# Two modulation dots per swiglu tile behind the tile's low part, one per output tile, their loads on GpSimd's queue

## The chip, the cores and the metric

The program runs on one core of one Trainium2 chip. The metric is the device time of one execution in microseconds; the profile's span is the time from the first to the last instruction of one execution. TensorE does the matmuls, VectorE, ScalarE and GpSimd the elementwise work, and DMA queues move the data: SP's queue (SyncE) here carries nearly all loads, GpSimd's queue the indirect ones.

## What is computed

Two model blocks on 512 tokens of width 1024. The first has two layers (a gated linear attention, then a latent attention), each followed by a swiglu; the second has a pooling branch beside a convolution branch, and then a layer that picks experts. Each layer is modulated by a vector `mod` that comes from the condition `c` alone, not from the tokens. Cut to what matters here:

```python
D_FF = 2816
for i in range(2):
    mod = c_act @ ada_w[i] + ada_b[i]                 # c_act = silu(c), 1024 -> 6144
    sh1, sc1, g1, sh2, sc2, g2 = jnp.split(mod, 6, axis=-1)
    x = x + g1[:, None, :] * mixer_i(modulate(x, norm_mix[i], sh1, sc1))
    h = modulate(x, norm_ffn[i], sh2, sc2)
    gate, up = jnp.split(h @ ffn_w_in[i], 2, axis=-1)
    x = x + g2[:, None, :] * ((silu(gate) * up) @ ffn_w_out[i])
# the second block begins with mod = silu(c_2) @ ada_w_2 + ada_b_2
```

## The kernel before

The tokens lie along the free dimension: an activation is eight tiles of 128 x 512. A matmul with full precision is made of three in float32r (`mm3`, L274 to L276): activations and weights are each split into a high and a low part, the high part by a ScalarE cast, the low part by a VectorE subtraction (`split`, L240). Weights come in units of 128 x 2048 (`raw<-wst`, 1 MB, from SP's queue, two buffers); each unit is cut into two halves, `whi` and `wlo`, with four buffers each. One unit holds 16 blocks of 128 x 128.

A swiglu (`ffn`, twice in the program) runs in two halves of eleven hidden tiles. For each tile TensorE makes the gate and the up product (8 blocks each, so one unit of weights and 48 matmuls), ScalarE takes the silu of the gate (L739), VectorE multiplies it with the up product (`s`, L741), ScalarE makes the high part `fh` and VectorE the low part `fl` (both L240). Then follow the output tiles of that half: each sums eleven k (33 matmuls), in the order of the hidden tiles, and VectorE adds the result to x (`residual`, L448). The first half has eight output tiles. The second half has six, then `tail` makes the last two with the norm of the next layer, in two halves of the tokens, and `ahead` begins the next layer's matmuls, with the weight low parts on GpSimd.

The modulation vectors are no matmuls: each column of 128 values is one VectorE instruction over 128 x 1024 with an accumulated sum (L312, a dot; `dot`), on a tile `araw` of 0.5 MB that has two buffers. `ada` (L314 to L324) is a generator that does one load and one dot at each `step()`. It is side work: layer 0's last piece (8 dots) and all of layer 1 (48 dots) run beside the first swiglu, those of the second block (48) beside the second swiglu; `silu_c(1)` loads c_2 into the buffer `sc` of the dots and takes its silu on ScalarE (L306, L307) once layer 1's dots have read it. The steps of one kind run in order, each dot in VectorE's program order.

The order of the instructions on each engine is fixed when the program is built, by a scheduler that goes by program order and by a simulated readiness; `tc.issue_after(ins)` forces what a block issues on the engine of `ins` to stand behind it. Before, each tile calls three steps, whose dots have to stand only behind the norm's last instruction, so the scheduler places them by itself.

Of the kernel before, what the change touches and what calls it, by code (L numbers as in the profile page):

```python
# [17 lines left out]
ALU = mybir.AluOpType  # L18
# [3 lines left out]
P = 128  # L22
# [38 lines left out]
ST = (3, 2, 2)  # L61
ARAW = 2
APART = 4
FST = 3
SPILL = [NA // 2 + (2 * i + 1) * (P // 2 - NA // 2) // (2 * NSP) for i in range(NSP)]
LAST = 2
GSC = 2.0 ** 14
# [126 lines left out]
def block_kernel(ctx, tc, x_in, cs_in, wst, vec, cst, gmask, smask, pos, ada1, ada2, wgate, keys, ust, uex, vex, out):  # L194
    nc = tc.nc
    V, A_, T_, G_, SP = nc.vector, nc.scalar, nc.tensor, nc.gpsimd, nc.sync
# [10 lines left out]
    def bank(tag="mm"):  # L207
        return ps.tile([P, S], F32, tag=tag, bufs=4, name=tag)
# [17 lines left out]
    x = [keep.tile([P, S], F32, name=f"x{k}") for k in range(KD)]  # L226
# [10 lines left out]
    state = {"i": 0, "pre": [], "ahead": 0}  # L237

    def split(hi, lo, src, eng=None):
        state["split"] = (A_.copy(hi, src), (eng or V).tensor_sub(lo, src, hi.bitcast(F32)))  # L240
# [16 lines left out]
    def blk(name, n=1, eng=None):  # L257
        while SEQ[state["i"]][0] == "pad":
            state["i"] += 1
        i = state["i"]  # L260
        assert SEQ[i][0] == name, (SEQ[i], name)
        u, o = divmod(i, UB)
        assert o + n <= UB
        if state.get("u") != u:
            with tc.high_priority(state["ahead"]):
                raw = wp.tile([P, UB * P], F32, tag="raw", bufs=RAW, name="raw")
                SP.dma_start(raw, wst[u])
                state["w"] = parts(raw, G_ if name in POOL_LO else eng)
            state["u"] = u
        state["i"] = i + n  # L270
        return part(state["w"], o * P, n * P)

    def mm3(out_, wh, wl, ah, al, first, last):
        T_.matmul(out_, wh, ah, start=first, stop=False)  # L274
        T_.matmul(out_, wh, al, start=False, stop=False)  # L275
        state["mm"] = T_.matmul(out_, wl, ah, start=False, stop=last)  # L276
# [4 lines left out]
    def ahead(name, ah, al):  # L281

        ws = [[blk(name, eng=G_) for _ in ah] for _ in range(4)]
        pre = [bank("mm" if i < 3 else "acc") for i in range(4)]
        for half in range(2):
            cs = halves(half)
            for p, w in zip(pre, ws):
                for k, (wh, wl) in enumerate(w):
                    mm3(p[:, cs], wh, wl, ah[k][:, cs], al[k][:, cs], k == 0, k == len(ah) - 1)
        state["pre"] = pre  # L290

    def proj(name, ah, al, tag="mm"):
        if state["pre"]:
            return state["pre"].pop(0)
        p = bank(tag)
        n = len(ah)
        for k in range(n):
            wh, wl = blk(name)
            mm3(p, wh, wl, ah[k], al[k], k == 0, k == n - 1)
        return p  # L300
# [9 lines left out]
    def dot(out_, w, sc, op=V.scalar_tensor_tensor):  # L310

        op(out=w, in0=w, scalar=1.0, in1=sc, op0=ALU.mult, op1=ALU.mult, accum_out=out_)  # L312

    def ada(l, w, sc, bias, pieces=range(6)):  # L314

        for p in pieces:
            for n in range(p * KD, (p + 1) * KD):
                raw = mn.tile([P, D], F32, tag="araw", bufs=ARAW, name="araw")
                SP.dma_start(raw, w[n * P:(n + 1) * P, :])
                dot(mods[l][:, n:n + 1], raw, sc)  # L320
                if n % KD == KD - 1:
                    m = mods[l][:, p * KD:(p + 1) * KD]
                    V.tensor_add(m, m, bias[:, p * KD:(p + 1) * KD])
                yield  # L324
# [3 lines left out]
    def step(n=1):  # L328
        for _ in range(n):
            next(side["g"], None)  # L330

    def rest():
        for _ in side["g"]:
            pass
# [97 lines left out]
    def tail(name, ah, al, gate, sqs, norm):  # L432

        ws = [[blk(name) for _ in ah] for _ in range(2)]
        for half in range(2):
            cs = halves(half)
            for i, w in enumerate(ws):
                n = KD - 2 + i
                p = bank()
                for k, (wh, wl) in enumerate(w):  # L440
                    mm3(p[:, cs], wh, wl, ah[k][:, cs], al[k][:, cs], k == 0, k == len(ah) - 1)
                residual(n, p, gate, cs)
                for sq, scale in sqs:
                    sq.add(x[n], scale=scale and scale(n), half=half)
            norm(half)

    def residual(n, p, gate, cs=slice(0, S)):
        V.scalar_tensor_tensor(x[n][:, cs], p[:, cs], gate[:, n:n + 1], x[n][:, cs], op0=ALU.mult, op1=ALU.add)  # L448

    def output_norm(name, ah, al, gate, gain, shift, first):  # L450

# [12 lines left out]
    with tc.tile_pool(name="st", bufs=1, reuse_waits="tile") as st, tc.high_priority(2 * AHEAD):  # L464
# [42 lines left out]
        def weights():  # L507
            with ExitStack() as s:
                for eng in (A_, G_):
                    if eng in last:  # L510
                        s.enter_context(tc.issue_after(last[eng].ins))
                state["split"] = None
                w = [blk("gla_w_in", eng=G_) for _ in pre]
                if state["split"]:
                    last[A_], last[G_] = state["split"]
            return w
# [10 lines left out]
        w = weights()  # L527
# [9 lines left out]
        for k in range(KD):  # L537
# [11 lines left out]
            w = w_  # L549
# [4 lines left out]
    with tc.tile_pool(name="gla", bufs=1, reuse_waits="tile") as gp:  # L554
# [19 lines left out]
        p = proj("gla_w_in", hh, hl)  # L574
# [4 lines left out]
        def gates():  # L579

            az, mz = [], []
            for h in range(GLA_H):
                z = bank("acc")
                T_.matmul(z, wg[:, h * P:(h + 1) * P], glr, start=True, stop=True)
                bg = vc("gla_b_gate", h)
                a = gp.tile([P, S], F32, tag="b", bufs=4, name="az")
                m = gp.tile([P, S], F32, tag="vn", bufs=8, name="mz")
                A_.activation(a, z, AF.Abs, bias=bg)
                V.tensor_scalar(m, z, bg, 0.0, op0=ALU.add, op1=ALU.min)
                az.append(a)  # L590
                mz.append(m)
            for a in az:
                e = A_.activation(a, a, AF.Exp, scale=-1.0)
            with tc.issue_after(e.ins):
                for h in range(GLA_H):
                    n = A_.activation(az[h], az[h], AF.Ln, bias=1.0)
                    V.tensor_sub(mz[h], mz[h], az[h])
                    V.tensor_tensor_scan(az[h], smk, mz[h], 0.0, op0=ALU.mult, op1=ALU.add)
            return az, n
# [102 lines left out]
        bs, n = gates()  # L702
        for what in GLA_ORDER.split():
# [8 lines left out]
            elif kind == "r":  # L712
                p = proj("gla_w_in", hh, hl)
# [15 lines left out]

    def ffn(l, sqs, norm, first):  # L730
        gate = mods[l][:, 40:48]
        norm_ = state["norm"]
        with tc.tile_pool(name=f"ffn{l}", bufs=1, reuse_waits="tile") as fp:
            for half in range(2):
                fh, fl = [], []
                for i in range(11):
                    p = proj("ffn_w_in", hh, hl)
                    s = fp.tile([P, S], F32, tag="s", bufs=2, name="s")
                    A_.activation(s, p, AF.Silu)  # L739
                    p = proj("ffn_w_in", hh, hl)  # L740
                    V.tensor_mul(s, s, p)  # L741
                    a = fp.tile([P, S], F32R, name=f"fh{i}")
                    c = fp.tile([P, S], F32R, name=f"fl{i}")
                    split(a, c, s)
                    fh.append(a)
                    fl.append(c)
                    with tc.issue_after(norm_.ins):
                        step(FST)
                for n in range(KD - 2 * half):
                    residual(n, proj("ffn_w_out", fh, fl), gate)  # L750
                    if half:
                        for sq, scale in sqs:
                            sq.pool = sq.pool or fp
                            sq.add(x[n], scale=scale and scale(n))
            rest()
            tail("ffn_w_out", fh, fl, gate, sqs, norm)
            ahead(first, hh, hl)
# [207 lines left out]
    for half in range(2):  # L965
        cs = halves(half)
# [5 lines left out]
    with tc.tile_pool(name="b2", bufs=1, reuse_waits="tile") as bp:  # L972
# [4 lines left out]
        for n in range(4):  # L977
            p = proj("w_in_2", hh, hl)
# [5 lines left out]
        for n in range(4):  # L984
            p = proj("w_in_2", hh, hl)
# [34 lines left out]
        for g in range(4):  # L1020
            p = proj("w_in_2", hh, hl)
            step(4)
            w = WINDOWS[g]
# [20 lines left out]
        for n in range(16):  # L1044
            p = proj("w_in_2", hh, hl)
# [10 lines left out]
        for g in range(4):  # L1056
            p = bank("mm")
# [26 lines left out]
        for n in range(8):  # L1084
            p = proj("pool_up_2", ph_, pl_)
            V.tensor_mul(sg[n], sg[n], p)
        for n in range(8):
            p = proj("conv_out_2", ch_, cl_)
# [9 lines left out]
    with tc.tile_pool(name="peer", bufs=1, reuse_waits="tile") as pp:  # L1098
# [38 lines left out]
        with tc.tile_pool(name="sel", bufs=1, reuse_waits="tile") as sp:  # L1137
# [179 lines left out]
            for h in range(PH):  # L1317
                qq, ql = [], []
                for half in range(2):
                    p = proj("w_query_2", hh, hl)  # L1320
                    t = sp.tile([P, 3 * P], F32, tag="q", bufs=4, name="q")
                    A_.copy(t, p[:, :S - P])
                    l = sp.tile([P, P], F32, name=f"ql{h}_{half}")
# [3 lines left out]
                for c in range(NT - 1):  # L1327
                    cs = slice(c * P, (c + 1) * P)
# [21 lines left out]
        with tc.tile_pool(name="exp", bufs=1, reuse_waits="tile") as ep:  # L1350
# [81 lines left out]
            for g in range(P // GJ):  # L1432
# [13 lines left out]
                for half in range(2):  # L1446
# [12 lines left out]
                    for dd in range(4):  # L1459
                        n = half * 4 + dd  # L1460
# [95 lines left out]
```

## Time and profile before

| | |
|---|---|
| median of three runs | 2837.29 us (2834.54 to 2839.94) |
| the profiled execution | 2844.19 us, span 2842.3 us |
| TensorE busy | 2716.3 us (96%) |
| VectorE busy | 2109.8 us (74%) |
| ScalarE busy | 1070.5 us (38%) |
| GpSimd busy | 704.0 us (25%) |
| DMA moved | 560.62 MB, 197 GB/s in the mean |
| first swiglu, from the first product to its norm | about 338 to 685 us |
| second swiglu | about 944 to 1290 us |

Times are those of one profiled execution unless a run is named. Busy time of TensorE is modelled: the durations of its matmuls overlap, so the rate is read from the distance between the starts of neighbouring rows. In a timeline's row, the square bracket gives the idle time of the engine just before the instruction and what ended it. In a list of waits, the columns are the waiting instruction, what it waited for, the total in us, how often, and the longest.

### The profile page before, as it was taken

The page shows a single profiled execution, that of the slowest core. Times are in us where ns is not written, and L with a number is a line of the kernel's source. Part 1 is how long each engine was busy: PE and PEld are TensorE (multiplying, and loading weights), DVE is VectorE, ACT ScalarE, POOL GpSimd, SP SyncE. Part 2 cuts the span into 40 slices and gives each one's busy share as a digit, 9 for nine tenths or more (in the row PEclk, how much of TensorE's full clock was granted, in tenths as well). Part 3 has the DMA queues.
Part 4 walks back from the last instruction along what each step waited for, and adds up shares of the span by engine and source line. Part 5 has one row for each costly group of instructions (what it writes and reads, how often), then busy time and mean ns, then how long its engine had stood idle before and what let it go on. Part 6 is the DMA issues. An engine that isn't in the chain of part 4 may idle for free. (4 is left out here: it accounts for less than half of the span.)

```text
span 2842.3 us, 38989 instructions
## 1 busy us (share of the span) xinstructions
PE 2716.3 (96%) x14889; PEld 2441.4 (86%) x14889; DVE 2109.8 (74%) x4011; ACT 1070.5 (38%) x1530; POOL 704.0 (25%) x556
## 2 busy tenths in 40 slices
PE   6789998999999999999999999998899999999998
PEld 4677887888778878888888889998899999999998
DVE  8874766435776774337966798888989898988986
ACT  4443322222433322233453336653333333333332
POOL 4541100001011000001521420003545455444550
PEclk9899999999999999999999999999999999999999
DMA  6441477422211674232223236656999998998993
GB/s 267 139 137 62 148 259 256 142 95 88 75 45 60 210 264 148 89 104 76 89 89 104 77 120 214 210 196 241 337 340 359 355 340 328 341 344 320 350 344 131
DMA packets 184363, 560.62 MB, mean 197 GB/s; under 512 B 13248, under 2 KB 66912, under 8 KB 157680
## 3 DMA queue, kind: packets, MB, share of 16 engines
q1 hardware_dynamic: 142352, 407.08, 40.9%
q0 software_dynamic: 41472, 151.01, 14.3%
q8 instruction: 117, 1.92, 0.3%
q14 instruction: 70, 0.57, 0.1%
q10 hardware_dynamic: 352, 0.03, 0.0%
HBM read 527.32 MB, written 30.75 MB: 196 GB/s over the span
## 5 line engine op out<-in xcount | busy, mean ns | idle before, releaser
L240 ACT CAST whi<-raw 128x1024 fp32r<-128x1024 f32 x510 | 535.6, 1051 | 1171.4 <-PE mm L275 689.7
L275 PE MATMUL mm<-hl,whi 128*128 128x512 f32 (+2 forms) x2544 | 899.8, 355 | 8.9 <-DVE hl L426 8.1
L274 PE MATMUL mm<-hh,whi 128*128 128x512 f32 (+2 forms) x2544 | 899.7, 355 | 2.7 <-ACT hh L425 2.0
L276 PE MATMUL mm<-hh,wlo 128*128 128x512 f32 (+2 forms) x2544 | 898.8, 354 | 0.1
L240 DVE TENSOR_TENSOR wlo<-raw,whi 128x1024 fp32r<-128x1024 f32 x472 | 580.2, 1230 | 296.8 <-ACT whi L240 288.0
L275 PEld LDWEIGHTS mm<-hl,whi 128*128 128x128 f32 x2544 | 482.4, 190 | 57.4 <-DVE hl L426 9.8
L274 PEld LDWEIGHTS mm<-hh,whi 128*128 128x128 f32 x2544 | 482.5, 190 | 49.5 <-ACT hh L425 2.6
L276 PEld LDWEIGHTS mm<-hh,wlo 128*128 128x128 f32 x2544 | 482.8, 190 | 48.2 <-issue 1.5
L240 POOL TENSOR_TENSOR wlo<-raw,whi 128x1024 fp32r<-128x1024 f32 x38 | 90.7, 2391 | 908.7 <-ACT whi L240 864.0
L1377 POOL DMA_INDIRECT rows<-vex,eidx x144 | 215.2, 1494 | 214.4 <-DVE y L1391 198.1
L1377 POOL DMA_INDIRECT rows<-uex,eidx x144 | 210.1, 1459 | 214.2 <-DVE rows L1381 164.9
L312 DVE SCALAR_TENSOR_TENSOR araw<-araw,sc 128x1024 f32<-128x1024 f32 x128 | 160.6, 1258 | 98.0 <-DMA araw<-ada 97.4
L1391 DVE SCALAR_TENSOR_TENSOR y<-rows,act,y 128x1024 f32<-128x1024 f32 x142 | 181.7, 1280 | 7.3 <-DMA rows<-vex,eidx 6.7
L1381 DVE SCALAR_TENSOR_TENSOR rows<-rows,hn 128x1024 f32<-128x1024 f32 x144 | 170.1, 1220 | 14.8 <-DMA rows<-uex,eidx 14.8
L274 PE MATMUL mm<-fh,whi 128*128 128x512 f32 (+1 forms) x396 | 147.5, 372 | 11.3 <-ACT fh L240 11.3
L275 PE MATMUL mm<-fl,whi 128*128 128x512 f32 (+1 forms) x396 | 147.7, 373 | 1.7 <-DVE fl L240 1.7
L276 PE MATMUL mm<-fh,wlo 128*128 128x512 f32 (+1 forms) x396 | 146.9, 371 | 0.0
L1310 ACT ACTIVATE stage<-acc 128x512 f32<-128x512 f32 x92 | 91.6, 1105 | 37.0 <-PE acc L1307 26.6
L1307 PE MATMUL acc<-oa,ob 128*128 128x128 f16 x736 | 101.5, 296 | 0.3 <-DVE oa L1298 0.2
L274 PEld LDWEIGHTS mm<-fh,whi 128*128 128x128 f32 x396 | 76.2, 192 | 24.6 <-ACT fh L240 12.1
L448 DVE SCALAR_TENSOR_TENSOR x<-mm,mod,x 128x512 f32<-128x512 f32 (+1 forms) x66 | 43.9, 666 | 62.8 <-PE mm L276 62.7
L275 PEld LDWEIGHTS mm<-fl,whi 128*128 128x128 f32 x396 | 76.1, 192 | 15.3 <-DVE fl L240 2.7
(1381 smaller groups left out, 4593.9 us busy)
## 6 DMA issues: line engine op xcount, KB each, us to landing
raw<-wst SPq DMA_DIRECT2D x127, 1024.0 KB, 4.9
araw<-ada SPq DMA_DIRECT2D x128, 512.0 KB, 4.6
raw<-ust SPq DMA_DIRECT2D x64, 1024.0 KB, 6.4
raw<-vex SPq DMA_DIRECT2D x64, 1024.0 KB, 7.6
gd<-stage SPq DMA_DIRECT2D x23, 1024.0 KB, 4.5
gt<-gd SPq DMA_DIRECT2D x16, 1472.0 KB, 9.4
aw<-ada SPq DMA_DIRECT2D x16, 512.0 KB, 8.9
spilled<-a SPq DMA_DIRECT2D x24, 184.0 KB, 3.1
```

Source lines behind the costliest of these rows:

```text
L240: state["split"] = (A_.copy(hi, src), (eng or V).tensor_sub(lo, src, hi.bitcast(F32)))
L274: T_.matmul(out_, wh, ah, start=first, stop=False)
L275: T_.matmul(out_, wh, al, start=False, stop=False)
L276: state["mm"] = T_.matmul(out_, wl, ah, start=False, stop=last)
L312: op(out=w, in0=w, scalar=1.0, in1=sc, op0=ALU.mult, op1=ALU.mult, accum_out=out_)
L448: V.scalar_tensor_tensor(x[n][:, cs], p[:, cs], gate[:, n:n + 1], x[n][:, cs], op0=ALU.mult, op1=ALU.add)
L1307: T_.matmul(p[:, t * P:(t + 1) * P], ob[:, q, :, t], oa[i][:, q, :, t], start=i == 0, stop=i == 1)
L1310: A_.mul(st[:, :, t1:t1 + 4].rearrange("p j t -> p t j"), p.rearrange("p (t j) -> p t j", t=4), 1.0 / GSC)
L1377: G_.indirect_dma_start(out=r, out_offset=None, in_=uex if up_ else vex, in_offset=bass.IndirectOffsetOnAxis(ap=eidx[:, n:n + 1] if n < P ...
L1381: V.scalar_tensor_tensor(r, r, 1.0, hn if n < P else hx, op0=ALU.mult, op1=ALU.mult, accum_out=act[:, n:n + 1])
L1391: V.scalar_tensor_tensor(z, r, act[:, n:n + 1], z, op0=ALU.mult, op1=ALU.add)
```

## The change

Three edits. In a swiglu tile, two steps instead of three (`FST`), and their dots now stand behind the tile's own low part `fl` (the VectorE half of `split`) instead of the norm. Each output tile, except the last two, which `tail` makes, gets one step behind its residual. The loads of `ada` for layer 1 and for the second block go to GpSimd's queue; those of layer 0 stay on SP's.

```diff
-FST = 3
+FST = 2
@@ ada
-                SP.dma_start(raw, w[n * P:(n + 1) * P, :])
+                (G_ if l else SP).dma_start(raw, w[n * P:(n + 1) * P, :])
@@ residual
-        V.scalar_tensor_tensor(x[n][:, cs], p[:, cs], gate[:, n:n + 1], x[n][:, cs], op0=ALU.mult, op1=ALU.add)
+        return V.scalar_tensor_tensor(x[n][:, cs], p[:, cs], gate[:, n:n + 1], x[n][:, cs], op0=ALU.mult, op1=ALU.add)
@@ ffn
-        norm_ = state["norm"]
...
-                    with tc.issue_after(norm_.ins):
+                    with tc.issue_after(state["split"][1].ins):
                         step(FST)
                 for n in range(KD - 2 * half):
-                    residual(n, proj("ffn_w_out", fh, fl), gate)
+                    r = residual(n, proj("ffn_w_out", fh, fl), gate)
+                    with tc.issue_after(r.ins):
+                        step()
```

The lines after it move up by one in `ffn` (L741 becomes L740) and down by one behind it.

VectorE at the end of the first half of the first swiglu, before. `fl_3222` is tile 9's low part, `L741` the product of tile 10, `fl_3298` tile 10's low part; `L312` is a dot:

```order
L240 TENSOR_TENSOR fl_3222<-s,fh_3221 128x512
L312 SCALAR_TENSOR_TENSOR araw,mod_109<-araw,sc 128x1024 x2
L240 TENSOR_TENSOR wlo<-raw,whi 128x1024
L312 SCALAR_TENSOR_TENSOR araw,mod_109<-araw,sc 128x1024 x2
L741 TENSOR_TENSOR s<-s,mm 128x512
L240 TENSOR_TENSOR wlo<-raw,whi 128x1024
L240 TENSOR_TENSOR fl_3298<-s,fh_3297 128x512
```

The same place on VectorE in the change, where tile 9's low part is `fl_3194` and tile 10's `fl_3267`:

```order
L240 TENSOR_TENSOR fl_3194<-s,fh_3193 128x512
L312 SCALAR_TENSOR_TENSOR araw,mod_109<-araw,sc 128x1024 x2
L240 TENSOR_TENSOR wlo<-raw,whi 128x1024
L740 TENSOR_TENSOR s<-s,mm 128x512
L240 TENSOR_TENSOR wlo<-raw,whi 128x1024
L240 TENSOR_TENSOR fl_3267<-s,fh_3266 128x512
```

Two of the four dots that stood ahead of tile 10's product now stand behind later instructions; the order of the other rows is the same.

GpSimd, from the end of the first mixer to the start of the second block, before; `wlo` are the low parts that `ahead` makes, `qs` belongs to the latent attention:

```order
L607 TENSOR_TENSOR qi<-qi,q 128x512
L682 TENSOR_TENSOR o<-sr,o 128x512 x8
L240 TENSOR_TENSOR wlo<-raw,whi 128x1024 x8
L881 TENSOR_TENSOR qs<-qr,qs 64x512 x8
L240 TENSOR_TENSOR wlo<-raw,whi 128x1024 x8
```

The same stretch of GpSimd in the change:

```order
L682 TENSOR_TENSOR o<-sr,o 128x512 x8
L240 TENSOR_TENSOR wlo<-raw,whi 128x1024 x4
L319 DMA araw<-ada 128x1024 x50
L240 TENSOR_TENSOR wlo<-raw,whi 128x1024 x4
L882 TENSOR_TENSOR qs<-qr,qs 64x512 x8
L240 TENSOR_TENSOR wlo<-raw,whi 128x1024 x4
L319 DMA araw<-ada 128x1024 x46
L240 TENSOR_TENSOR wlo<-raw,whi 128x1024 x4
```

Of each group of eight low parts, the first four now stand ahead of the loads and the last four behind them.

SP's queue around the end of the first swiglu's dots, before; `raw` are weight units, `sc` is c_2, `posi` is the first load of the latent attention:

```order
L319 DMA araw<-ada 128x1024 x4
L267 DMA raw<-wst 128x2048
L306 DMA sc<-cs_in 128x1024
L319 DMA araw<-ada 128x1024 x2
L267 DMA raw<-wst 128x2048 x17
L772 DMA posi<-pos 128x512
```

The same queue in the change, from the last loads of layer 0 on:

```order
L319 DMA araw<-ada 128x1024 x2
L267 DMA raw<-wst 128x2048
L319 DMA araw<-ada 128x1024 x2
L267 DMA raw<-wst 128x2048 x27
L306 DMA sc<-cs_in 128x1024
L267 DMA raw<-wst 128x2048 x2
L773 DMA posi<-pos 128x512
```

The weight units follow one another without dot loads between them, and c_2's load stands two weight units ahead of `posi` instead of seventeen.

## Rows read from the trace of the kernel before

**Rows 1.** View: waits in the first swiglu (325 to 700 us).

```profile
ACT fh L240 <- DVE s L741: 62.3, 10, 11.2
DVE araw L312 <- DMA araw<-ada: 52.4, 42, 5.6
...
PE mm L274 <- ACT fh L240: 7.4, 1, 7.4
```

**Rows 2.** View: timeline of TensorE, first swiglu, first output tile: start, duration, instruction.

```profile
445.28 0.39 PE L276 MATMUL mm<-fh,wlo 128*128 128x512 f32 x1
453.08 0.79 PE L274 MATMUL mm<-fh,whi 128*128 128x512 f32 x1 [7.41 <-ACT fh L240]
...
459.95 0.39 PE L274 MATMUL mm<-fh,whi 128*128 128x512 f32 x1
...
465.17 0.39 PE L276 MATMUL mm<-fh,wlo 128*128 128x512 f32 x1
...
469.93 0.39 PE L276 MATMUL mm<-fh,wlo 128*128 128x512 f32 x1
```

**Rows 3.** The same view in the second swiglu.

```profile
1050.98 0.39 PE L276 MATMUL mm<-fh,wlo 128*128 128x512 f32 x1
1055.24 0.79 PE L274 MATMUL mm<-fh,whi 128*128 128x512 f32 x1 [3.88 <-ACT fh L240]
...
1064.12 0.40 PE L276 MATMUL mm<-fh,wlo 128*128 128x512 f32 x1
```

**Rows 4.** View: busy time by window: length, five engines, granted clock, DMA share, GB/s.

```profile
502.00:515.00 13.00, 13.00 (x59) 10.78 (x58) 6.41 (x10) 2.95 (x3) 0.00 (x0) 1.00 0.74 248
...
1051.00:1064.00 13.00, 7.68 (x19) 5.42 (x18) 9.22 (x15) 1.57 (x2) 0.00 (x0) 0.61 0.72 253
```

**Rows 5.** View: timeline of VectorE, first swiglu, ahead of the gap.

```profile
439.26 0.68 DVE L240 TENSOR_TENSOR fl<-s,fh 128x512 fp32r<-128x512 f32 x1
...
449.32 1.23 DVE L312 SCALAR_TENSOR_TENSOR araw<-araw,sc 128x1024 f32<-128x1024 f32 x1 [5.62 <-DMA araw<-ada]
...
451.69 0.68 DVE L741 TENSOR_TENSOR s<-s,mm 128x512 f32<-128x512 f32 x1
```

**Rows 6.** The page: the dots, busy and mean, idle before them.

```profile
L312 DVE SCALAR_TENSOR_TENSOR araw<-araw,sc 128x1024 f32<-128x1024 f32 x128 | 160.6, 1258 | 98.0 <-DMA araw<-ada 97.4
```

**Rows 7.** View: timeline of VectorE, first swiglu, second half, tiles without dots.

```profile
618.67 0.69 DVE L741 TENSOR_TENSOR s<-s,mm 128x512 f32<-128x512 f32 x1 [3.38 <-PE mm L276]
...
620.60 0.69 DVE L240 TENSOR_TENSOR fl<-s,fh 128x512 fp32r<-128x512 f32 x1
624.95 1.23 DVE L240 TENSOR_TENSOR wlo<-raw,whi 128x1024 fp32r<-128x1024 f32 x1 [3.66 <-ACT whi L240]
629.55 0.69 DVE L741 TENSOR_TENSOR s<-s,mm 128x512 f32<-128x512 f32 x1 [3.38 <-PE mm L276]
```

**Rows 8.** Views of line L1377 (indirect loads) and tile araw: ns, and landing, least/median/most.

```profile
L1377 POOL DMA_INDIRECT rows<-uex,eidx x144: 934/1677/1990, 1956.1 to 2355.8; - x144
...
DMA to landing us min/median/max: 4.2/7.4/12.0
...
DMA to landing us min/median/max: 3.2/4.6/8.4
```

**Rows 9.** View: timelines of GpSimd and VectorE at the first swiglu's norm.

```profile
686.19 2.35 POOL L240 TENSOR_TENSOR wlo<-raw,whi 128x1024 fp32r<-128x1024 f32 x1 [9.84 <-DVE ry L357]
...
686.20 2.35 DVE L355 TENSOR_TENSOR rt<-ry 128x2 f32<-128x2 f32 x1
688.59 0.16 DVE L356 TENSOR_TENSOR rt<-rt,rv 128x2 f32<-128x2 f32 x1
```

**Rows 10.** View: timeline of ScalarE at the silu of c_2.

```profile
511.28 1.06 ACT L307 ACTIVATE sc<-sc 128x1024 f32<-128x1024 f32 x1 [11.53 <-DMA sc<-cs_in]
```

**Rows 11.** View of line L1381, VectorE's dots on the indirect loads: ns, least/median/most.

```profile
L1381 DVE SCALAR_TENSOR_TENSOR rows<-rows,hn x144: 1209/1220/1228, 1965.0 to 2369.4; 128x1024 f32<-128x1024 f32 x144
```

**Rows 12.** The page: GB/s moved in 40 equal slices of the span.

```profile
GB/s 267 139 137 62 148 259 256 142 95 88 75 45 60 210 264 148 89 104 76 89 89 104 77 120 214 210 196 241 337 340 359 355 340 328 341 344 320 350 344 131
```

## The prediction

> **What bounds the kernel now.** I read the page first: TensorE is busy for 96% of the span, so a change to VectorE's work is worth only what it gives back in TensorE's gaps. The second view is the list of waits for the stretch of the first swiglu (325 to 700 us). It shows one TensorE wait of 7.4 us, on ScalarE's high part fh, and behind it ScalarE waiting for VectorE's product s, ten times, 62.3 us in all [rows 1]. The third view is TensorE's timeline. Where the rows run undisturbed, the 22 matmuls from 465.17 to 469.93 take 21 steps of 0.2267 us [rows 2]. Everything from 334 to 685 us keeps that step, except at one place: after 445.28 the next matmul starts at 453.08, and the full step is back only at 459.95 [rows 2]. That is the first output tile of the first half, at its eleventh and last k: thirty matmuls use tiles 0 to 9, and the next one needs tile 10. The second swiglu has the same hole: 1050.98, then 1055.24, and the full step again by 1064.12 [rows 3]. The granted clock in that stretch is 0.61 on average, against 1.00 undisturbed [rows 4], so the matmuls behind the gap start at about half the rate, at the lower of the two levels.
>
> VectorE's timeline says why tile 10 is late [rows 5]. Tile 9's low part is written at 439.26. Then come four modulation dots (L312) and one weight low part, and only at 451.69 tile 10's product. One of the four had waited 5.62 us for its load (start 449.32). The waits of these dots for their loads are 97.4 us over the program [rows 6], 52.4 of them in this swiglu [rows 1]. The work that VectorE does there is not too much; it stands in a queue behind a load.
>
> **What the two holes cost.** First: from 445.28 to 459.95 are 16 steps, 14.67 us against 16 x 0.2267 = 3.63, so 11.04 us lost, of it 7.6 in the gap and the rest at the lower clock. Second: from 1050.98 to 1064.12 are 18 steps, 13.14 against 4.08, so 9.06 us lost. Together 20.1 us. That is all that these two stages can give at this point; the small gaps at the end of each swiglu (the norm) are not touched.
>
> **The change, part by part.**
>
> Two dots per tile, and behind the tile's own low part. By the order, there were four dots between tile 9's low part and tile 10's product, and there are two now. In a half whose tiles have no dots (the second half of the first swiglu) one tile takes 629.55 - 618.67 = 10.88 us, and VectorE is idle twice in it: 3.66 us between the low part (620.60 + 0.69 = 21.29) and the next weight low part at 624.95, and 3.38 us ahead of the next product [rows 7]. Two dots of 1.23 us fill 2.46 of the first 3.66. Per tile VectorE then has 0.69 + 1.23 + 0.69 + 1.23 + 2.46 = 6.3 us of 10.88. In that half TensorE needs tile 10 in the same way and shows no gap. Its cover: ten k before it are 30 x 0.2267 = 6.8 us from the end of the up product, while the low part is done 620.60 + 0.69 - 618.67 = 2.6 us after the product starts; some 4 us are to spare, and VectorE's 3.38 us of idle time ahead of the product come on top. So if the two loads are there, both holes close: **-20.1 us**. Bounds: 0 (the wait takes another shape) and -20.1.
>
> One dot behind each output tile. Before, the order has all 56 dots of the first swiglu done in its first half; now 30 stand in the first half (22 and 8), 22 in the second half's tiles and 4 behind its first output tiles. The second swiglu has 48, now 30 and 18. The gate that the residuals need is the first eight dots; they are done with the fourth tile. Each dot adds 1.23 us to an output tile of 33 x 0.2267 = 7.5 us in which VectorE has one residual and some 1.4 weight parts. Cost: 0. All dots are done before the last two output tiles and the norm, where VectorE is on the path; were one left there, it would cost its 1.23 us.
>
> Loads of layers 1 and 2 from GpSimd's queue. 96 of 104 loads leave SP's queue, where the order has three or four of them ahead of each weight load; the eight of layer 0 stay. GpSimd is idle in this stretch (0.00 in the windows) [rows 4]. No plain load from GpSimd is in the trace. The nearest rows are its indirect loads of the same 128 x 1024 tile late in the program: 0.93 to 1.99 us of GpSimd's time in the first 144, and 4.2 / 7.4 / 12.0 us to landing (least, median, most); from SP these loads took 3.2 / 4.6 / 8.4 [rows 8]. What decides is the turnaround of a buffer: there are two, each is used once per tile, so load plus dot must fit 10.88 us, that is, the load may take 9.65 us. I take 7.4, since it is GpSimd's own median, under heavier traffic than here; 4.6 to 12.0 go into the range. At 7.4 there are 2.2 us to spare, and the cost is 0. Gone ahead of the weight loads on SP, they could let those start earlier, but no TensorE wait was put down to a weight load here: gain 0.
>
> GpSimd's own work behind these loads. In its queue 50 loads now stand ahead of the last four weight low parts of the first swiglu (46 in the second), which start TensorE's next stage. The last of these loads waits for the last dot of layer 1, behind the fourth output tile of the second half; the first low part that TensorE's next stage waits for ran at 686.19, within the norm [rows 9]. Three output tiles of 7.5 us lie between: 22 us of cover. Cost: 0.
>
> ScalarE's silu of c_2 follows the last dot of layer 1, so it moves from the gap at 500 us to the second half's output tiles. In the old place ScalarE stood 11.53 us for that load, up to 511.28 [rows 10], while TensorE ran through (13.00 of 13.00 us from 502 on) [rows 4]. In the new place its neighbours are the squares of the norm; three output tiles, 22 us, still follow. Cost: 0; if the cover failed, at most the few us by which the load lands late.
>
> A port. GpSimd's weight low part at 686.19 and a 128 x 2 VectorE instruction at 686.20 took the same 2.35 us; the next such instruction took 0.16 [rows 9]. So two engines can hold each other up. Beside 144 indirect loads from GpSimd, however, VectorE's dot of two SBUF tiles took 1209 / 1220 / 1228 ns [rows 11]: nothing of it. The Trainium skill ("SBUF — State Buffer", "Who interferes with whom") says that a VectorE instruction with two SBUF inputs blocks, or is blocked by, a GpSimd instruction that reads SBUF, and that loads issued by GpSimd starve while VectorE runs a copy, cast or tensor_scalar in a two-port mode. The rows agree with the first half; VectorE has none of the second kind in these tiles, and no run here shows that starvation. By that rule alone the sum stays as it is.
>
> **The rivals.**
>
> Late loads, partly (B). GpSimd's loads land at 9 to 10 us, a dot still stands in front of tile 10's product, and half of the loss remains: 10 us gained, 2827. For it: landings up to 12.0 [rows 8]. Against: these came where some 340 GB/s were moved [rows 12]; two loads of 0.524 MB and one of 1.049 MB per 10.88 us are 193.
>
> Another wait takes its place (C). Tile 10 is on time, and TensorE stops elsewhere in the same stage for as long: 2837. Against: the dotless half shows no gap at all with the same rest of the order [rows 4, 7].
>
> Turnaround becomes the bound (D), slower. With a load of L us a tile lasts L + 1.23 once that passes 10.88, in some 40 tiles. It starts at L = 9.65 and eats the whole gain at 20.1 / 40 = 0.5 us a tile, L = 10.15. At L = 11 it costs 40 x 1.35 = 54 us: 2837 - 20 + 54 = 2871. For it: the 12.0. Against: the median 7.4, and that not all 40 tiles would meet the worst.
>
> **How the numbers follow.** The profiled execution took 2844.19 us (span 2842.3); 2844.19 - 20.1 = 2824.1, a change of 0.71%. On the median 2837.29 that is 2837.29 x 0.9929 = 2817.2. Chances: forecast 0.72, B 0.14, C 0.08, D 0.06. 0.2%, or 5.7 us, is about what a measurement of this kernel can tell from no change. Faster by more: the forecast and most of B, 0.83; same: C and the smallest B, 0.11; slower: D, 0.06. The three runs of before lie 5.4 us apart, so the forecast alone spans 2812 to 2823; with B and the fast side of C the range is 2812 to 2832. D's long side and the rest of C lie outside.
>
> **What would show it.** In the changed profile: no TensorE gap at the first output tile of either first half, and the clock at 1.00 there; the dots' wait for loads down from 97.4 us to under 20; 96 loads on GpSimd with a landing between 4.6 and 7.4 us; the software queue up by 96 x 0.524 = 50 MB. If the gap is there and a dot waits for its load ahead of tile 10's product, B is right; if tiles last longer than 10.88 us all along, D; if TensorE waits for whi, wlo or the norm instead, C. I am wrong at the root if the holes close and the time does not move.

## The result, and the profile after

| | before | after |
|---|---|---|
| median | 2837.29 us (2832.46 to 2848.37) | 2821.91 us (2817.87 to 2822.92) |
| ratio after / before | | 0.994, 95% interval 0.9924 to 0.9956 |
| median, in a second group of runs (E9) | 2839.24 us | 2819.85 us (2815.48 to 2823.82) |
| ratio there | | 0.9929, 95% interval 0.9914 to 0.9944 |
| span of the profiled execution | 2842.3 us | 2820.3 us (clock 0.986 in the mean, before 0.981) |

The kernel is 15 to 19 us faster. The profiled executions differ by 22.0 us (that of before lies 6.9 us above the median of its runs, that of after 0.2), and where they differ is plain: if the two traces are laid beside each other instruction by instruction (ScalarE's casts), the distance is -11.1 us from the first output tile of the first swiglu on, -13.0 from the norm behind the latent attention on (920 us of before), -22.1 from the first output tile of the second swiglu on, and -22.0 at the end.

The waits of TensorE after, 325 to 700 us (columns: who waited for what, us in all, times, longest). The wait on `fh` of [rows 1] is gone; what is left belongs to the norm, and stood there before as well:

```profile
PE acc L369 <- DVE ry L357: 3.1, 3, 2.4
PE mm L275 <- DVE hl L426: 2.1, 2, 1.9
PE mm L274 <- ACT hh L425: 0.4, 1, 0.4
```

Busy time by window, after, around the first output tile of either first half (columns as in [rows 4]). TensorE is busy all through at a granted clock of 1.00 (its higher level, 2.4 GHz), where [rows 4] has 7.68 of 13.00 us and 0.61:

```profile
440.00:460.00 20.00, 20.00 (x90) 16.54 (x89) 11.61 (x17) 3.43 (x4) 2.12 (x4) 1.00 0.64 211
1045.00:1064.00 19.00, 19.00 (x85) 15.75 (x84) 9.43 (x13) 3.17 (x4) 1.37 (x3) 1.00 0.50 171
```

VectorE's timeline after, tile 10 of the first swiglu, which answers to [rows 5]. The product is on time: the bracket says that VectorE stood idle for 3.38 us until TensorE was done, the same 3.38 as in tiles without dots [rows 7]:

```profile
438.94 0.69 DVE L740 TENSOR_TENSOR s<-s,mm 128x512 f32<-128x512 f32 x1 [3.38 <-PE mm L276]
439.73 1.23 DVE L240 TENSOR_TENSOR wlo<-raw,whi 128x1024 fp32r<-128x1024 f32 x1
440.87 0.68 DVE L240 TENSOR_TENSOR fl<-s,fh 128x512 fp32r<-128x512 f32 x1
441.47 1.22 DVE L312 SCALAR_TENSOR_TENSOR araw<-araw,sc 128x1024 f32<-128x1024 f32 x1
...
442.61 1.22 DVE L312 SCALAR_TENSOR_TENSOR araw<-araw,sc 128x1024 f32<-128x1024 f32 x1
...
445.21 1.23 DVE L240 TENSOR_TENSOR wlo<-raw,whi 128x1024 fp32r<-128x1024 f32 x1 [1.36 <-ACT whi L240]
```

The page after: the dots and their loads (busy and mean | idle before them), and the issues (KB each, us to landing). The dots' wait for loads is 5.5 us where [rows 6] has 97.4:

```profile
L312 DVE SCALAR_TENSOR_TENSOR araw<-araw,sc 128x1024 f32<-128x1024 f32 x128 | 157.1, 1251 | 5.6 <-DMA araw<-ada 5.5
...
L319 POOL DMA_DIRECT2D araw<-ada x96 | 51.1, 533 | 555.4 <-DVE araw L312 538.1
...
araw<-ada POOLq DMA_DIRECT2D x96, 512.0 KB, 4.6
...
araw<-ada SPq DMA_DIRECT2D x32, 512.0 KB, 4.3
```

### The profile page after: what moved, and what is told of

Read it like the earlier page. It is cut to its first block, busy times and chain, and to the rows that moved or that the text cites. A ratio compares the mean times of both kernels' runs of the same rounds, so it can differ in the third digit from the quotient of the medians.

```text
span 2820.3 us, 38954 instructions
## 1 busy us (share of the span) xinstructions
PE 2706.4 (96%) x14889; PEld 2435.0 (86%) x14889; DVE 2107.8 (75%) x4011; ACT 1072.3 (38%) x1530; POOL 759.5 (27%) x652
## 5 line engine op out<-in xcount | busy, mean ns | idle before, releaser
L319 POOL DMA_DIRECT2D araw<-ada x96 | 51.1, 533 | 555.4 <-DVE araw L312 538.1
L312 DVE SCALAR_TENSOR_TENSOR araw<-araw,sc 128x1024 f32<-128x1024 f32 x128 | 157.1, 1251 | 5.6 <-DMA araw<-ada 5.5
L740 DVE TENSOR_TENSOR s<-s,mm 128x512 f32<-128x512 f32 x42 | 28.9, 688 | 133.6 <-PE mm L276 133.0
```

What stands on the lines that cost most here:

```text
L319: (G_ if l else SP).dma_start(raw, w[n * P:(n + 1) * P, :])
```

## A second reading of the trace before: late a little in every tile

The prediction explained the hole by what stands directly ahead of tile 10's product. VectorE's timeline over the whole half shows something else. Three products of before follow; none has a bracket, so VectorE came to each of them straight from another instruction, and they stand 12.03 and 11.87 us apart, where TensorE needs 10.88 (all the distances of that half from the second tile on lie between 9.75 and 14.17 us):

```profile
391.18 0.68 DVE L741 TENSOR_TENSOR s<-s,mm 128x512 f32<-128x512 f32 x1
...
403.21 0.68 DVE L741 TENSOR_TENSOR s<-s,mm 128x512 f32<-128x512 f32 x1
...
415.08 0.68 DVE L741 TENSOR_TENSOR s<-s,mm 128x512 f32<-128x512 f32 x1
```

After, each stands 10.88 us behind the last, with the same idle time ahead of it:

```profile
417.18 0.69 DVE L740 TENSOR_TENSOR s<-s,mm 128x512 f32<-128x512 f32 x1 [3.38 <-PE mm L276]
428.06 0.69 DVE L740 TENSOR_TENSOR s<-s,mm 128x512 f32<-128x512 f32 x1 [3.38 <-PE mm L276]
```

What takes 12 us is in the load buffers. Before, a tile has four dots on two buffers, so each buffer is turned round twice. SP's queue before, a load into the first buffer:

```profile
369.83 0.33 SPq L319 DMA_DIRECT2D araw<-ada  x1
```

VectorE before, the dot that used it:

```profile
374.50 1.23 DVE L312 SCALAR_TENSOR_TENSOR araw<-araw,sc 128x1024 f32<-128x1024 f32 x1 [1.37 <-DMA araw<-ada]
```

SP's queue before, the next load into that buffer:

```profile
375.76 0.33 SPq L319 DMA_DIRECT2D araw<-ada  x1
```

From the issue to its dot 4.67 us, and 1.23 for the dot: from one issue to the next, one turn, are 5.93 us, and two are 11.9. VectorE takes its instructions in order, so the product waits behind the dots. After, with two dots a tile, no buffer is turned round within a tile, and a load has a whole tile's time.

Two explanations of the hole are thus to be told apart. **Place** is the prediction's: the dots between tile 9's low part and tile 10's product, one of them waiting 5.62 us. **Lag** is this: some 1.1 us more a tile in the mean of ten tiles, summed until TensorE's cover is used up. In the expectations of the first four runs T is the turnaround of the buffers, Q the queue of the loads and P the place.

The trace before already weighs the two. In the first swiglu, 7.8 of the 11.1 us by which tile 10 is late were there at tile 9's product, and 3.3 came in the stretch that the prediction read. In the second swiglu all of it was there (10.2 us at tile 9, 9.2 at tile 10): two dots, not four, stand between tile 9's low part and tile 10's product, and this last distance is 9.85 us. VectorE before, the products of tiles 9 and 10 of the second swiglu:

```profile
1044.00 0.68 DVE L741 TENSOR_TENSOR s<-s,mm 128x512 f32<-128x512 f32 x1
...
1053.85 0.68 DVE L741 TENSOR_TENSOR s<-s,mm 128x512 f32<-128x512 f32 x1
```

## The experiments

Each ratio is to runs of the kernel before on the same chip (medians 2838.33, 2837.38 and 2839.24 us in the three groups E1 to E4, E5 to E8, E9 to E12).

**E1, the loads back on SP's queue.**

```diff
-                (G_ if l else SP).dma_start(raw, w[n * P:(n + 1) * P, :])
+                SP.dma_start(raw, w[n * P:(n + 1) * P, :])
```

> The change with all loads of the dots back on SP's queue; the order on VectorE is that of the change. Theory T (turnaround): the holes come from how often a load's buffer has to turn around per tile; two dots on two buffers need one turnaround of load plus dot (4.7 + 1.2 us, at most 8.1 + 1.2) in a tile of 10.88 us, so the queue is idle talk: no hole at the first output tiles, time as the change, 2817 to 2824 us. Rival Q (queue): loads behind weight units on SP come late, a hole of several us returns, 2828 to 2838 us.

2823.15 us, ratio 0.9947 (0.9927 to 0.9967). No hole, products 10.88 us apart, the dots wait 6.4 us for loads, landing 4.4 us in the median of all 128 loads (after: 4.5). As far as these intervals tell, the gain is the whole gain without the change of queue. VectorE of E1, tile 10's product:

```profile
441.69 0.69 DVE L740 TENSOR_TENSOR s<-s,mm 128x512 f32<-128x512 f32 x1 [3.38 <-PE mm L276]
```

**E2, the kernel before with its loads on GpSimd's queue**: the one line of E1 the other way, in the kernel before.

> The kernel before with only the loads of layer 1 and of the second block moved to GpSimd's queue; three steps per tile behind the norm, which the scheduler makes into four dots per tile on two buffers. Theory T: two turnarounds a tile, 2 x (4.7 + 1.2) = 11.8 us against 10.88, so products slip by about 1 us a tile as before, both holes stay, 2830 to 2842 us. Rival Q: GpSimd's own queue gets the loads there in time, holes gone or below 2 us, 2817 to 2824 us.

2854.21 us, ratio 1.0054 (1.0035 to 1.0073): 15.9 us slower than before, and 12 above the end of T's range. The holes are still there, larger. TensorE's timeline of E2:

```profile
445.18 0.39 PE L276 MATMUL mm<-fh,wlo 128*128 128x512 f32 x1
456.81 0.80 PE L274 MATMUL mm<-fh,whi 128*128 128x512 f32 x1 [11.23 <-ACT fh L240]
```

The products are 12.6 to 13.25 us apart in the seven tiles ahead of it, so the lag is some 2 us a tile instead of 1.2. GpSimd of E2, one issue:

```profile
368.96 0.53 POOL L319 DMA_DIRECT2D araw<-ada  x1 [2.95 <-DVE araw L312]
```

VectorE of E2, the end of the dot that freed the buffer, and the dot that used it next (this load took longer than most):

```profile
368.58 0.08 DVE L312 DVE_READ_ACCUMULATOR araw<-araw,sc 128x1 f32 x1
...
375.41 1.23 DVE L312 SCALAR_TENSOR_TENSOR araw<-araw,sc 128x1024 f32<-128x1024 f32 x1 [2.85 <-DMA araw<-ada]
```

GpSimd starts its issue 0.30 us after the accumulator is read (368.66); SP started 0.03 us after (369.80, then 369.83). The landing of the loads in this half, counted from the issue, was 4.8 us in the median against 4.7. That is some 0.37 us a turn, twice a tile: 0.7 of the 0.8 us by which a tile is longer than before (12.9 against 12.1 in the mean of these seven). The Trainium skill ("Trainium Kernel Development and Optimization", "Key Constraints") says that DMAs of the SP, ACT and POOL queues run on the same 16 DMA engines, and that several issuers only save issue time. E1 agrees (4.4 against 4.5 us in the median from issue to landing, over all 128 loads), and E2 shows the issuer's own delay, which is hidden with two dots a tile and not with four.

**E3, the changed kernel with one load buffer** (`ARAW = 1`, so for the loads ahead of the swiglus too).

> The change with one buffer for the loads instead of two. Theory T: two dots a tile on one buffer are again two turnarounds, 2 x (4.6 + 1.2) = 11.6 us or more, so products come 11.6 to 12.2 us apart in every half with two dots per tile (first and second half of the first swiglu, first half of the second, most of its second half); holes at the end of three or four halves, 2830 to 2865 us. Rival P (place): only that two dots stand behind the tile's own low part matters, products stay 10.88 us apart, 2817 to 2824 us.

2830.38 us, ratio 0.997 (0.9955 to 0.9984): about half the gain is gone. Two dots on one buffer are two turns again; products stand up to 12.13 us apart, in the second swiglu mostly 11.3 to 11.8. T had said 11.6 to 12.2 in every half and a hole in three or four of them. There are two holes, and in the first swiglu most products are 10.88 us apart: with one load under way at a time, its landing took 3.9 us in the median instead of the 4.6 that T took, and by the same working two turns are 2 x (0.3 + 3.9 + 1.2) = 10.8 us, an estimate that lies just at TensorE's 10.88. In both holes TensorE waits for the low part, which now stands behind a late dot. VectorE of E3, ahead of the second hole:

```profile
1042.57 1.22 DVE L312 SCALAR_TENSOR_TENSOR araw<-araw,sc 128x1024 f32<-128x1024 f32 x1 [2.55 <-DMA araw<-ada]
...
1043.72 0.69 DVE L240 TENSOR_TENSOR fl<-s,fh 128x512 fp32r<-128x512 f32 x1
```

**E4, the kernel before with four load buffers in the swiglus**: nothing is moved by hand, and the tile `araw` in `ada` gets `bufs=4` from the swiglu's pool.

> The kernel before (three steps per tile behind the norm, loads on SP) with four buffers for the loads within the swiglus instead of two; the scheduler then makes it four to five dots a tile. Theory T: a tile needs 5/4 of a turnaround, some 7.5 us, so products are 10.9 us apart from where the dots have caught up and the holes shrink to under 3 us each, though VectorE then works 3.8 + 5 x 1.2 = 10 us of a tile; 2815 to 2827 us. Rival P (place and number of dots): four or five dots ahead of tile 10's product still make it late, 2832 to 2842 us.

2827.92 us, ratio 0.9968 (0.9956 to 0.998). The first hole is closed, the second is 2.2 us, and the dots wait 34.2 us instead of 97.4. The median lies 0.9 us above T's range. With four buffers a load takes longer to land (5.8 us in the median, before 4.6), and still the lag is gone in the first swiglu. VectorE does four dots or more in a tile there, so it is not the number of dots that made it late. Buffers alone, with the dots still where the scheduler puts them, bring 10.4 us, more than half of the gain.

**E5, the changed kernel with four dots ahead of tile 10's product** and two everywhere else (`LASTX = 2`, `LASTT = 10`): the direct test of Place.

```diff
-                        step(FST)
+                        step(FST + (LASTX if not half and len(fl) == LASTT else 0))
```

> The changed kernel with two more dots behind tile 9's low part in the first half of each swiglu, so that four dots stand ahead of tile 10's product, as in the kernel before, while every earlier tile keeps two. Place (the prediction's own step): the hole at the first output tile is made by the dots that stand between tile 9's low part and tile 10's product, so it comes back, at about 8 and 4 us with the low clock behind them: 2835 to 2842. Lag (what the first four experiments point to): VectorE was late there because every tile of the half with four dots took 1 to 1.3 us more than TensorE's 10.88, summed over nine tiles; four dots in the last tile alone make it late by 1 to 2 us, which the banks in hand cover: no hole over 2.5 us, 2820 to 2826.

2822.36 us, ratio 0.9947 (0.9931 to 0.9964), and TensorE has no gap at either first output tile: Place falls. VectorE of E5 (its lines stand two lower: L314 is the dot, L742 the product, L242 the low part):

```profile
429.19 0.69 DVE L742 TENSOR_TENSOR s<-s,mm 128x512 f32<-128x512 f32 x1 [3.38 <-PE mm L278]
...
431.12 0.69 DVE L242 TENSOR_TENSOR fl<-s,fh 128x512 fp32r<-128x512 f32 x1
431.73 1.22 DVE L314 SCALAR_TENSOR_TENSOR araw<-araw,sc 128x1024 f32<-128x1024 f32 x1
...
432.87 1.22 DVE L314 SCALAR_TENSOR_TENSOR araw<-araw,sc 128x1024 f32<-128x1024 f32 x1
...
438.69 1.23 DVE L314 SCALAR_TENSOR_TENSOR araw<-araw,sc 128x1024 f32<-128x1024 f32 x1 [2.00 <-DMA araw<-ada]
...
439.93 1.23 DVE L314 SCALAR_TENSOR_TENSOR araw<-araw,sc 128x1024 f32<-128x1024 f32 x1
...
441.08 0.68 DVE L742 TENSOR_TENSOR s<-s,mm 128x512 f32<-128x512 f32 x1
```

The same four dots as in [rows 5], and one waits for its load, but tile 10's product is only 1.01 us late (11.89 behind the one before it), because VectorE came to this tile on time (3.38 us idle ahead of tile 9's product). The load was waited for 2.00 us here and 5.62 in [rows 5]; with the 3.62 us more, an estimate, the product would be 4.6 us late, against 11.1 before.

**E6, three dots behind each low part, none at the output tiles** (`FST = 3`, the step behind the residual taken out).

> The changed kernel with three dots behind each tile's own low part and none with the output tiles. Lag: two load buffers turn round in about 6 us, so three dots need one and a half turns, 9 us, which is under TensorE's 10.88: products 10.88 us apart, no hole, 2820 to 2826. Place: three dots are 3.7 us ahead of tile 10's product against 3.66 us that VectorE had idle there, and a late load adds to it: a hole of 0 to 5 us in each swiglu, 2823 to 2833.

2833.59 us, ratio 0.9984 (0.9974 to 0.9995): nearly all of the gain is gone, and my price for three dots (one and a half turns, 9 us) was wrong. In the number Place came nearer (2823 to 2833); what speaks for Lag is the spacing of the products below. GpSimd of E6 in the second swiglu:

```profile
1001.67 0.53 POOL L319 DMA_DIRECT2D araw<-ada  x1 [2.95 <-DVE araw L312]
```

VectorE of E6, the three dots of that tile and the first of the next:

```profile
1000.15 1.22 DVE L312 SCALAR_TENSOR_TENSOR araw<-araw,sc 128x1024 f32<-128x1024 f32 x1
...
1002.09 1.23 DVE L312 SCALAR_TENSOR_TENSOR araw<-araw,sc 128x1024 f32<-128x1024 f32 x1 [0.71 <-DMA araw<-ada]
...
1008.71 1.23 DVE L312 SCALAR_TENSOR_TENSOR araw<-araw,sc 128x1024 f32<-128x1024 f32 x1 [4.25 <-DMA araw<-ada]
...
1012.20 1.22 DVE L312 SCALAR_TENSOR_TENSOR araw<-araw,sc 128x1024 f32<-128x1024 f32 x1
```

The third dot of a tile needs the buffer of the first. It starts 7.0 us after that buffer's issue and holds up the product, the weight low part and `fl`, and only behind these comes the next tile's first dot, at 1012.20. In order that is a full turn plus the tile's own work, 12.05 us; in the first swiglu the last eight distances are 11.4 us in the mean, in the second 11.6. TensorE waits 5.48 us at the first output tile of the second swiglu, at 1045.97, and not at all at that of the first.

**E7, two steps a tile, held behind the norm alone as before** (`issue_after(norm_.ins)`): the scheduler then puts four dots into each early tile and none into the last ones.

> The changed kernel with its dots held behind the norm alone, as before: two steps for each tile, but the order puts four into each of the first four tiles and none into the last five. Lag: the products of the early tiles stand 12 us or more apart and VectorE falls 4 to 6 us behind, then catches up in the tiles without dots, so that it is on time at the first output tile: no hole, 2820 to 2827. If being behind costs at once (TensorE waiting for a bank in the early tiles), there are gaps near 360 to 400 us and the time is 2827 to 2838. Place: no dot stands ahead of tile 10's product, no hole, 2820 to 2826; what tells is the spacing of the early products.

2827.53 us, ratio 0.9961 (0.9947 to 0.9976). VectorE falls behind in the early tiles, so that the products at 391.20 and 401.42 are 5 to 6 us late, and then it catches up within a tile, as VectorE's timeline of E7 shows:

```profile
401.42 0.68 DVE L741 TENSOR_TENSOR s<-s,mm 128x512 f32<-128x512 f32 x1
...
405.51 0.69 DVE L741 TENSOR_TENSOR s<-s,mm 128x512 f32<-128x512 f32 x1 [0.54 <-PE mm L276]
...
416.39 0.69 DVE L741 TENSOR_TENSOR s<-s,mm 128x512 f32<-128x512 f32 x1 [3.38 <-PE mm L276]
```

No hole at either first output tile. The median lies 0.5 us above Lag's range, and the trace can't say why: the six executions took 2818.7, 2819.1 and 2827.3 to 2829.4 us, and the profiled one is 2819.1. A small cost elsewhere stays open.

**Lateness and hole.** From the trace of each kernel: how much longer the time from tile 0's product to tile 10's is than in the changed kernel (102.83 and 102.06 us), and TensorE's waits at the first output tile (us, first swiglu / second):

| kernel | late by | TensorE waits |
|---|---|---|
| before | 11.1 / 9.2 | 7.7 / 5.3 |
| E2 | 15.7 / 20.3 | 11.5 / 11.4 |
| E3 | 2.5 / 5.8 | 1.6 / 4.9 |
| E4 | -1.1 / 5.3 | 0 / 2.2 |
| E5 | 1.0 / 0.4 | 0 / 0 |
| E6 | 4.3 / 10.8 | 0 / 5.8 |
| E7 | -1.6 / 0.0 | 0 / 0 |

The wait is the lateness less 3 to 5 us, whatever made it late; the prediction had some 4 us as TensorE's cover. E3, where a dot also stands ahead of `fl`, has less cover (about 1 us). In E2's second swiglu, 20.3 us late, TensorE had waited another 2.6 us in the tiles and ahead of the output tile; the rest of that difference stays open.

**E10, the changed kernel without the step at the output tiles.**

> The changed kernel without the step at each output tile: two dots behind each tile's low part, in both halves, and what is left of the 96 behind the swiglu. Lag: two dots a tile never turn a buffer round within a tile, so the first output tile has no hole; the output tiles' dots were hidden, so taking them away gains nothing: 2818 to 2827, unless the 8 to 10 dots that are left over at the end of each swiglu stand in the norm's chain, then up to 10 us more: 2828 to 2838. The output tiles' dots cost something: below 2818.

2824.51 us, ratio 0.9957 (0.9941 to 0.9973), against 2819.85 for the changed kernel beside it (E9). No hole in the halves, but dots are left for the end of the first swiglu, and ScalarE's silu of c_2 comes behind the last of them, among the squares of the norm. ScalarE of E10:

```profile
672.32 1.06 ACT L307 ACTIVATE sc<-sc 128x1024 f32<-128x1024 f32 x1 [6.09 <-DMA sc<-cs_in]
673.28 1.03 ACT L240 CAST whi<-raw 128x1024 fp32r<-128x1024 f32 x1
674.21 0.62 ACT L384 ACTIVATE sq<-x 128x512 f32<-128x512 f32 x1
```

TensorE of E10, its wait for VectorE's sum of these squares:

```profile
680.11 1.01 PE L362 MATMUL acc<-iv,sa 128*128 128x1 f32 x4 [8.90 <-DVE sa L395]
```

In the changed kernel the same silu stands at 655.25 and waits 3.40 us, and TensorE does not wait for it. So the step at each output tile costs nothing that these runs can tell, and it gets the dots done before the norm needs ScalarE and VectorE. Whether that gains time is not shown: this execution of E10, with the wait of 8.90 us, is 5.3 us behind the changed kernel's trace after the norm (counted from where the two stood ahead of it), but its span ends 1.6 us earlier, and the two intervals (0.9941 to 0.9973 and 0.9914 to 0.9944) just overlap.

**E9, the changed kernel again, and E8, E11, E12: the weight low parts that GpSimd makes ahead of a norm, on VectorE instead.**

```diff
-        ws = [[blk(name, eng=G_) for _ in ah] for _ in range(4)]
+        ws = [[blk(name) for _ in ah] for _ in range(4)]
```

E8 and E12 have this line; E11 has it only for the calls behind the two swiglus.

> The changed kernel itself, beside the next three on the same chip. Lag: as its first timing, 2818 to 2826, no hole at a first output tile, products 10.88 us apart.

> The changed kernel with the weight low parts of the weights got ready ahead of each norm (38 of them on GpSimd, 2.35 to 2.41 us each) on VectorE instead. Port: where GpSimd's low part meets a small VectorE instruction, that instruction also takes 2.3 us; without these the norms' chains are shorter by up to 2.3 us at some of the five places, and TensorE waits less there: 2812 to 2820. Load: VectorE takes 1.14 us for each instead and is itself the chain at the norm, so the chain grows by as much or more: 2822 to 2835.

> The changed kernel with the weight low parts that are made ahead of the norm on VectorE behind the two swiglus alone, and on GpSimd in the other places. In the run with all of them on VectorE the norm's chain behind the swiglus ended 2.5 and 6 us earlier than in the changed kernel's trace, and 1 to 2 us later behind the other norms. Port: those gains stay and the losses go, 2811 to 2819. If those offsets were chance from run to run: as the changed kernel, 2818 to 2826.

> The changed kernel with all 38 of these weight low parts on VectorE, beside the changed kernel on the same chip. Port: again 3 to 5 us under the changed kernel, 2813 to 2820. Chance of another chip or call: within 2 us of the changed kernel.

E9 2819.85 us (ratio 0.9929), E8 2817.33 (0.9927, 0.9914 to 0.994), E12 2817.71 (0.9923, 0.9909 to 0.9938), E11 2817.46 (0.9925, 0.991 to 0.9939). E11 and E12 lie 2.4 and 2.1 us under E9, beside which they ran, and all the intervals overlap almost wholly; whether they gain anything can't be told from these runs. I tried them because the profiled execution gained 1.9 us at a place that the change does not touch. GpSimd before, at the norm behind the latent attention:

```profile
914.49 2.34 POOL L240 TENSOR_TENSOR wlo<-raw,whi 128x1024 fp32r<-128x1024 f32 x1 [7.02 <-DVE rt L356]
```

VectorE before, 0.01 us later:

```profile
914.50 2.35 DVE L357 SCALAR_TENSOR_TENSOR ry<-rt,ry 128x2 f32<-128x2 f32 x1
```

TensorE before, waiting for that result:

```profile
916.99 0.66 PE L369 MATMUL acc<-ct,ry 128*128 128x128 f32 x2 [2.23 <-DVE ry L357]
```

GpSimd after, at the same place:

```profile
903.31 2.41 POOL L240 TENSOR_TENSOR wlo<-raw,whi 128x1024 fp32r<-128x1024 f32 x1 [7.02 <-DVE rt L356]
```

VectorE after, where the low part met the next instruction instead:

```profile
903.31 0.16 DVE L357 SCALAR_TENSOR_TENSOR ry<-rt,ry 128x2 f32<-128x2 f32 x1
903.58 2.42 DVE L395 TENSOR_TENSOR sa<-sa,sq 128x256 f32<-128x256 f32 x1
```

TensorE takes `ry` without that wait here, but 3.4 us later it waits 1.42 us for ScalarE's `hh`, so the place gives 1.9 us and not 2.23. The small VectorE instructions follow one another by 0.2 us, and the low part starts within 0.01 us of one in both traces; which instruction is caught hangs on less than that distance. The Trainium skill ("SBUF — State Buffer", "Who interferes with whom") has a VectorE instruction with two SBUF inputs contend with a GpSimd instruction that reads SBUF; the rows agree, with 2.35 us in place of 0.16.

## Why the prediction was right, and where not

The number. Forecast 2817.2 in 2812 to 2832; measured 2821.91 and 2819.85, a ratio of 0.994 and 0.9929 where 0.9929 was forecast; the forecast gain of 20.1 us lies within both intervals. Between the profiled executions the two holes gave back 11.1 and 9.1 us, the forecast terms were 11.04 and 9.06. The 1.9 us on top came at the norm, where the rows above show the port's accident; that this is all of its cause is argued, not shown.

**The step that was wrong** is the paragraph that says why tile 10 is late. It read VectorE from 439.26 to 451.69 only [rows 5], found four dots and one wait of 5.62 us, and made these the cause. E5 has the four dots there and no hole, and the second swiglu of before has the hole with two dots there. The lateness was gathered over ten tiles, and [rows 1] had said so: 42 waits, 52.4 us, of which the argument used one. The sum came out right all the same, because it was taken from TensorE's rows (what the hole costs) and not from its cause, and because the dotless half showed that an on-time VectorE leaves no hole. That the change also fitted the true cause was in part luck: two dots a tile were chosen to thin out the place ahead of tile 10, and the same edit brought each buffer to one turn a tile, which the prediction looked at only as a risk of the change.

Turnaround: the rule used for the changed kernel (each buffer once a tile, load plus dot within 10.88 us) is the one that the runs bear out. The load took 4.6 us, the lower bound, not the 7.4 I took; spacing and time show that it did not matter. Applied to the kernel before (twice a tile), the same rule would have given the 12 us a tile at once.

The queue: cost 0 was right as far as the runs can tell (E1), and it holds for two dots a tile only; with four it costs 15.9 us (E2).

The output tiles' dots: cost 0 was right as far as the runs can tell. That ScalarE's silu stays covered was right too, and these dots are why: E10, without them, shows the case named there, a load that lands late in the norm, with TensorE waiting 8.90 us in that trace.

The rivals: B and C did not come; the small waits that are left are the norm's. D's mechanism, a tile as long as a buffer's turn, does not decide the changed kernel, but it is what made the kernel before slow and E2 slower, and what took gain away in E3 and E6.

## What to carry to other kernels

When an engine is late at one point, read its rows back to where it was last on time (here: a product with a bracket of 3.38 us ahead of it) before naming a cause; the distance of like rows, tile by tile, tells a queue of a moment from a slip in every round. For side work on a few buffers, count how often a buffer must be turned round within one period of the bounding engine, in the order in which the waiting engine meets it: at one turn a period the load was free here, at more the turns add up and have to fit the period (two of 5.93 us did not fit 10.88; two of E3's shorter ones just about did), and moving the issue to another queue only added that issuer's delay. Side work that is left to the end of a stage can meet the next stage's first steps (E10); what that costs has to be measured.

## What the runs showed of the hardware that I had not expected

A load issued by GpSimd started 0.30 us after the instruction it waited for, one by SP 0.03 us after, and the issue took 0.53 against 0.33 us; the landing hardly differed (4.5 us in the median of all 128 loads with 96 of them on GpSimd's queue, 4.4 with all on SP's, E1). Two VectorE dots a tile hide that; four do not (E2). And the landing of these loads went with the number of buffers: 3.9 us in the median with one (E3), 4.5 with two (after), 5.8 with four in the swiglus (E4).
